# An mLSTM layer that forms the first head's values and gate columns ahead of its first queries, keys and output gates

## The chip, the cores and the metric

The kernel runs on one core of a Trainium2 chip. The metric is the device time of one execution in microseconds (us); where several runs are given, their median. The core has five engines with an instruction stream each: TensorE (PE in the rows, with its weight loads as PEld), VectorE (DVE), ScalarE (ACT), GpSimd (POOL) and SyncE (SP, which issues the transfers). They wait for one another through semaphores.

## The reference

The program is a trunk of four sub-layers on 1024 tokens of 1024 features: latent attention, a gated MLP, an mLSTM mixer ("matrix memory"), and a gated MLP again, each behind an RMS norm that is scaled and shifted by a conditioning vector. The change lies in the mLSTM mixer. Cut to what matters, it computes

```
proj = h @ w_in                       # h: normed input, 1024 x 1024
q, k, v, o, gates = split(proj)       # 4 heads; q, k 128 wide, v 256 wide a head
i_pre, f_pre = gates                  # one input and one forget gate a head and token
b = cumsum(log_sigmoid(f_pre))        # inside chunks
# a chunk after the other, with state C, n and running maximum m:
dmat  = b[t] - b[s] + i[s]            (causal)
m_t   = max(b + m, max(dmat))
s_mat = (q k^T) * exp(dmat - m_t)
num   = exp(b + m - m_t) * (C q) + s_mat v
den   = the same with n in place of C, and the row sums of s_mat
out   = num / max(|den|, exp(-m_t))
C, n, m = the state after the chunk
y = rms_norm(out) * head_norm * sigmoid(o);   result = y @ w_out
```

Values of all tokens are needed before a chunk's products, and the gates of all four heads come out of the same projection (eight columns of it).

## The kernel before, in words

Every matrix product in full precision is three matmuls (helper `mm3`, lines 178 to 180): the high and the low part of one operand with the high part of the other, and the high part with the low. A weight unit is a block of 128 x 1024 numbers: `unit` (lines 161 to 172) has SP load it into `wraw`, ScalarE copy it to its high part `whi` (line 170) and GpSimd subtract to get the low part `wlo` (line 171). The units' buffers rotate.

Tokens stand in two halves of 512. At the end of the MLP before, `norm_next` (lines 1109 to 1114) norms each half into `h[0]` and `h[1]`. For a half, ones are multiplied with the sums of squares `ssq` on TensorE (`st`, line 247), VectorE forms `var` (line 251), GpSimd `rstd` (line 252), TensorE spreads it over rows (`rb`, line 259), and then VectorE and ScalarE write eight blocks of h (lines 273 to 275). These TensorE steps do not stand where the code calls them. `later(n, step, key)` (line 190) puts a step in a queue, and `mm3` counts it down: the step is emitted after n more calls of `mm3`, that is 3n matmuls. `need(key)` (line 193) emits what is left of a key at once. For the second half `st` comes after W0 = 10 calls, and `rb` three calls later. The gate computation of the first head is placed in the same way by GATES: `gates0` (transposes `gg` of the gate columns `gtok`, then the chain of line 1366 to 1382 on ScalarE and VectorE), `gates1` (`gr`, lines 1386 and 1387), `gates2` (`gp`, line 1399), `gates3` (`gcol`, lines 1414 and 1415).

The mixer of head 0 begins with q, k and o of the first half (`in_proj`, 24 matmuls of 512 columns each, named `inp`), then `need(h[1])`, then q, k, o of the second half (72 matmuls), then eight tiles of values with the gates' columns (`vp`, 24 matmuls of 264 columns each, in the pool psA of four PSUM banks). Every `vp` is split into `va` by ScalarE and VectorE (lines 594, 595), and its last eight columns are copied to `gtok` (line 1345). Then come q and k of head 1 (`nxt = qk(1)`), five pieces of which (QK1) are emitted ahead of `need(gcol)`, and the chain over the chunks of head 0: `po` and `pc` with the state `C` (lines 1291 to 1297), with pieces of other projections between (`cover`), and `yT` at the head's end (line 1323).

All instructions of an engine run in one order, which the tile scheduler fixes when the kernel is built: an instruction stands about where it is emitted, and `tc.high_priority()` moves one ahead of other ready work of its engine.

Of the kernel before, what the change touches and what calls it, by code (L numbers as in the profile page):

```python
# [11 lines left out]
F32 = mybir.dt.float32  # L12
# [6 lines left out]
P = 128  # L19
D = 1024  # L20
S = 1024
KT = D // P
HS = 512
# [6 lines left out]
KSCALE = 128 ** -0.5  # L30
# [5 lines left out]
NT = 2  # L36

DVA = 258
QK1 = 5
SCALE_ACT = ((0, 0), (1, 0), (1, 1))  # L40

STEPS = "nspppnspppoooonmooso", "nnsposppooponpmspoopo"
# [1 line left out]
WARM = 14  # L44
W0, WF = 10, 12
SHARE = 7
GATES = (2, 16, 20, 24)
OUTS = 2
MODS = (0,) * 4 + (3,) + (2,) * 11
MODS_OUT = ((0,) * 5 + (1,) * 3, (1,) * 6 + (0,) * 2)  # L50
# [38 lines left out]
U_MQ, U_MK, U_MV, U_MO, U_MG, U_OUT1 = 0, 4, 8, 16, 24, 25  # L89
U_MV0 = (U_MV, U_MV + 1, U_MG)  # L90
# [10 lines left out]
def trunk_kernel(ctx: ExitStack, tc: tile.TileContext, xT, pos, c_d, cols_d, mod_w, win, winT, w0, w1, wf, wd, out):  # L101
    nc = tc.nc
    PSUM = bass.MemoryType.PSUM
    n_names = [0]

    def nm(s):
        n_names[0] += 1
        return f"{s}_{n_names[0]}"

    act, dve, pool, pe = nc.scalar, nc.vector, nc.gpsimd, nc.tensor  # L110
# [6 lines left out]
    def phase(name, **kw):  # L117
        st = ExitStack()
        p = st.enter_context(tc.tile_pool(name=name, bufs=1, reuse_waits="tile", **kw))
        return st, p  # L120
# [11 lines left out]
    def block(i, shape, dt, name):  # L132
        return blk.tile(shape, dt, tag=f"b{i}", name=nm(name))
# [27 lines left out]
    def mm_tile(name):  # L161
        return psA.tile([P, HS], F32, tag="mm", name=nm(name))


    def unit(src, lo_eng=None, w=1024):
        raw = wp.tile([P, 1024], F32, tag="wraw", bufs=wraws, name=nm("wraw"))[:, 0:w]
        nc.sync.dma_start(raw, src)
        hi = wp.tile([P, 1024], F32R, tag="whi", bufs=wbufs, name=nm("whi"))[:, 0:w]
        lo = wp.tile([P, 1024], F32R, tag="wlo", bufs=wbufs, name=nm("wlo"))[:, 0:w]
        act.activation(hi, raw, AF.Copy)  # L170
        (lo_eng or pool).tensor_tensor(lo, raw, hi.bitcast(F32), ALU.subtract)  # L171
        return hi, lo

    def mm3(ps, ls, rs, first, last, more=False):

        lh, ll = ls
        rh, rl = rs
        pe.matmul(ps, lh, rh, start=first, stop=False, skip_group_check=more)  # L178
        pe.matmul(ps[:, 0:rl.shape[-1]], lh, rl, start=False, stop=False, skip_group_check=more)  # L179
        pe.matmul(ps, ll, rh, start=False, stop=last, skip_group_check=more)  # L180
        for e in list(queue):
            e[0] -= 1
            if e[0] == 0:
                queue.remove(e)
                e[1]()
# [4 lines left out]
    def later(n, fn, key):  # L190
        queue.append([n, fn, key])

    def need(key):

        while any(e[2] is key for e in queue):
            e = next(e for e in queue if e[2] is key)
            queue.remove(e)
            e[1]()
# [94 lines left out]
    def halves(h, hf, k):  # L293
        return h[hf][0][:, k, :], h[hf][1][:, k, :]

    def wk(u, k, w=P):
        return u[0][:, k * w:(k + 1) * w], u[1][:, k * w:(k + 1) * w]
# [14 lines left out]
    h = [[block(2 + i, [P, KT, HS], F32R, "h") for i in range(2)], None]  # L312
# [7 lines left out]
    def small(name):  # L320
        return psS.tile([P, HS], F32, tag="sm", bufs=1, name=nm(name))
# [79 lines left out]
    ps = small("warm")  # L401
# [80 lines left out]
    def in_proj(u, hf):  # L482
        ps = mm_tile("inp")
        for k in range(KT):
            mm3(ps, wk(u, k), halves(h, hf, k), k == 0, k == KT - 1)
        return ps
# [105 lines left out]
    def split_ps(hi, lo, ps, scale=None):  # L592
        if scale is None:
            act.activation(hi, ps, AF.Copy)
            dve.tensor_tensor(lo, ps, hi.bitcast(F32), ALU.subtract)
        else:
            act.activation(hi, ps, AF.Copy, scale=scale)
            dve.scalar_tensor_tensor(lo, ps, scale, hi.bitcast(F32), ALU.mult, ALU.subtract)
# [173 lines left out]
    def piece(gen, n=1):  # L772
        for _ in range(n):
            next(gen, None)
# [3 lines left out]
    def proj_next():  # L778
        for r in proj:
            yield  # L780
            if r is not None:
                args.append(r)
                return
# [7 lines left out]
    for n in range(2 * NH):  # L791
        q, kk, qr, kvu, i, hf, head = args.pop(0)
        nxt = proj_next()
# [36 lines left out]
    def open_ffn(i):  # L830
        stX, px = phase("px", side="right")
        load_cols(i, px)
        stP = ExitStack()
        psC = stP.enter_context(tc.tile_pool(name="psC", bufs=1, space=PSUM, reuse_waits="tile"))
        return stX, px, stP, psC
# [254 lines left out]
    stX, px, stP, psC = open_ffn(1)  # L1090
# [34 lines left out]
    h = hs  # L1125
# [5 lines left out]
    def qk_tiles(hd):  # L1131

        if hd == 1:
            return [[ys[hf][:, t, :] for hf in range(2)] for t in (4, 6)]
        return [[pm.tile([P, HS], F32, tag=f"{t}{hf}", name=nm(t)) for hf in range(2)] for t in ("qT", "kT")]

    def qk_evac(ps, t, hf, scale):
        act.activation(t[hf], ps, AF.Copy, scale=scale)


    uqk = [unit(w1[U_MQ]), unit(w1[U_MK]), unit(w1[U_MO])]
    need(h[0])
    pqk = [in_proj(u, 0) for u in uqk]
    need(h[1])
    stP.close()
    stD.close()
    stX.close()

    stM, pm = phase("pm", side="right")
    stQ = ExitStack()  # L1150
    psD = stQ.enter_context(tc.tile_pool(name="psD", bufs=4, space=PSUM, reuse_waits="tile"))
    def og_evac(ps, m, hf):

        o = ys[hf][:, m, :]
        act.activation(o, ps, AF.Tanh, scale=0.5)
        pool.tensor_scalar(o, o, 0.5, 0.5, ALU.mult, ALU.add)

    ys = [block(XB[hf], [P, KT, HS], F32, "y") for hf in range(2)]
    qT, kT = qk_tiles(0)
    evacs = (lambda ps, hf: qk_evac(ps, qT, hf, 1.0), lambda ps, hf: qk_evac(ps, kT, hf, KSCALE),  # L1160
             lambda ps, hf: og_evac(ps, 0, hf))
    for ps, ev in zip(pqk, evacs):
        ev(ps, 0)
    for u, ev in zip(uqk, evacs):
        ev(in_proj(u, 1), 1)

    R = MH * NC

# [16 lines left out]
    def va_tiles():  # L1185

        hi, lo = [pm.tile([P, 8, w], F32R, tag=f"va{w}", name=nm("va")) for w in (DVA, 256)]
        pool.memset(hi[:, :, 256:DVA].bitcast(F32), 1.0)
        return hi, lo
# [44 lines left out]
    def load_rows(hd, hf):  # L1234

        o = (hd * NC + hf * 4) * P
        e, ib = crow[:, hf * HS:(hf + 1) * HS], pm.tile([P, HS], F32, tag="ib", name=nm("ib"))
        for i, t in enumerate((e, ib)):
            nc.sync.dma_start(t, g_d[i][:, o:o + HS].broadcast_to([P, HS]))
        grows.append((e, ib))  # L1240
# [86 lines left out]
    def run(gen):  # L1327
        while True:
            try:
                next(gen)  # L1330
            except StopIteration as e:
                return e.value


    gtok = pm.tile([P, 2 * MH, NC], F32, name="gtok")
    va = va_tiles()
    uv = [unit(w1[i]) for i in U_MV0]
    for t in range(8):
        ps = mm_tile("vp")
        tsl = slice((t % 4) * P, (t % 4 + 1) * P)  # L1340
        for k in range(KT):
            mm3(ps[:, 0:264], (h[t // 4][0][:, k, tsl], h[t // 4][1][:, k, tsl]), wk(uv[k // 3], k % 3, 264),
                k == 0, k == KT - 1)
        split_ps(va[0][:, t, 0:256], va[1][:, t, :], ps[:, 0:256])
        dve.tensor_copy(gtok[:, :, t], ps[:, 256:264])
    g1, g2 = crow[0:R, 0:4 * P], crow[0:R, 4 * P:8 * P]
    gi, gf, gb, gc = [g1[:, i * P:(i + 1) * P] for i in range(4)]
    ga, gu, gw, gl = [g2[:, i * P:(i + 1) * P] for i in range(4)]
# [8 lines left out]
    gcol = pm.tile([P, 4 * R], F32, name="gcol")  # L1357
# [53 lines left out]
    def gates3():  # L1411
# [5 lines left out]
        for hf in range(2):  # L1417
            load_rows(0, hf)

    for n, gate_step in zip(GATES, (gates0, gates1, gates2, gates3)):  # L1420
        later(n, gate_step, gcol)
    nxt = qk(1)
    piece(nxt, QK1)
    need(gcol)

    def gcl(kind, hd, c):
# [4 lines left out]
    for hd in range(MH):  # L1431
        pre, obs = [], []
        if hd == 0:
            steps = prep(hd, qT, kT, pre)
            next(steps)
            piece(nxt)
            run(steps)
            cover = (r for gen in (ogate(hd), nxt) for r in gen)
        else:
            vs = v_proj(hd) if hd > 1 else vs  # L1440
            va = next(vs)
            if hd > 1:
                piece(vs, 2)
            steps = prep(hd, qT, kT, pre)
            next(steps)
            piece(vs)
            run(steps)
            run(vs)
            cover = ogate(hd)
        for _ in chain(hd, pre, va, obs):  # L1450
            piece(cover)
        run(cover)
        if hd == 0:
            vs = v_proj(1)
            piece(vs, 2)
        elif hd < MH - 1:
            nxt = qk(hd + 1)
            piece(nxt, 2)
        finish(hd, obs)
        if hd < MH - 1:  # L1460
            run(nxt)
            qT, kT = qks.pop()
# [4 lines left out]
    stX, px, stP, psC = open_ffn(2)  # L1467
# [124 lines left out]
```

## Time and profile before

| | us |
|---|---|
| median of 3 runs | 2378.07 (2377.34 to 2380.62) |
| profiled execution, device time | 2385.82 |
| span in its profile | 2384.10 |
| TensorE busy in the span | 2276.5 (95%) |
| its idle in head 0's start, 1216.4 to 1336.1: `gr` | 4.0 |
| same stretch, `po` behind `C` | 1.9 and 0.6 |

The profile is one execution, whose time is 7.75 us over the median of the runs; a difference that is worked out from its rows is added to the median. Rows of the trace come in five views. The page gives totals. The waits view gives what an engine waited for: the engine and line that waited, the releaser behind the arrow, the sum, the number and the longest in us. The windows view gives busy time of each engine in a stretch. The timeline has one instruction a row, in brackets the idle time before it on its engine and what ended it. The transfer view lists the issues in a stretch.

### The profile page before, as it was taken

To read this page: it belongs to the slowest core of one execution; us is meant where nothing else is said; L and a number is where in the kernel's file an instruction comes from. 1 tells how busy PE (TensorE), PEld (TensorE's weight loads), DVE (VectorE), ACT (ScalarE), POOL (GpSimd) and SP (SyncE) were. 2 spreads that over 40 slices of the span, in tenths; PEclk is the share of its full clock that TensorE was granted. 3 is DMA by queue.
4 is the path that set the end of the run, shared out by engine and by line. 5 is a ranking of instruction groups with operands and counts; after the bars stand their busy time and mean duration, and the time that the engine had idled before them with its cause. 6 is when DMAs were issued, how large, how long until landed. Compare 5 with 4: busy or idle time off the path is not lost. (4 is left out here: it accounts for less than half of the span.)

```text
span 2384.1 us, 29447 instructions
## 1 busy us (share of the span) xinstructions
PE 2276.5 (95%) x10861; PEld 1897.2 (80%) x10861; DVE 1505.3 (63%) x2171; ACT 997.8 (42%) x1720; POOL 925.0 (39%) x626
## 2 busy tenths in 40 slices
PE   8999999997999999999999999999799999999997
PEld 6778888775788888788888888978578888878787
DVE  7777777589667666667864525366966666642515
ACT  5356556344444444433234324343444444442312
POOL 4221121435333333666532222234433333365644
PEclk8999999998999999999999999999899999999998
DMA  7512334833322222878652111163232222274533
GB/s 283 151 43 68 93 102 152 291 101 100 102 86 80 80 80 72 270 245 276 202 175 76 54 36 54 41 199 120 71 111 84 80 81 83 79 226 125 183 89 115
DMA packets 112896, 295.72 MB, mean 124 GB/s; under 512 B 13104, under 2 KB 16880, under 8 KB 112752
## 3 DMA queue, kind: packets, MB, share of 16 engines
q1 hardware_dynamic: 112752, 293.84, 38.5%
q8 instruction: 86, 1.41, 0.2%
q14 instruction: 58, 0.48, 0.1%
HBM read 246.70 MB, written 44.47 MB: 122 GB/s over the span
## 5 line engine op out<-in xcount | busy, mean ns | idle before, releaser
L171 POOL TENSOR_TENSOR wlo<-wraw,whi 128x1024 fp32r<-128x1024 f32 (+1 forms) x168 | 402.5, 2398 | 472.2 <-ACT whi L170 416.0
L170 ACT ACTIVATE whi<-wraw 128x1024 fp32r<-128x1024 f32 (+1 forms) x171 | 172.6, 1009 | 358.7 <-PE dn L179 159.0
L938 POOL TENSOR_TENSOR wlo<-raw,whi 128x512 fp32r<-128x512 f32 x132 | 195.7, 1487 | 276.7 <-ACT whi L937 267.7
L180 PE MATMUL dn<-u,wlo 128*128 128x512 f32 (+1 forms) x752 | 285.3, 379 | 1.3 <-POOL wlo L171 1.3
L178 PE MATMUL dn<-u,whi 128*128 128x512 f32 (+1 forms) x752 | 285.9, 380 | 0.0
L179 PE MATMUL dn<-u,whi 128*128 128x512 f32 (+1 forms) x752 | 285.4, 380 | 0.0
L178 PE MATMUL pa<-T,whi 128*128 128x512 f32 x528 | 210.7, 399 | 16.6 <-DVE a L1015 15.3
L179 PE MATMUL pa<-T,whi 128*128 128x512 f32 x528 | 210.1, 398 | 0.0
L180 PE MATMUL pa<-T,wlo 128*128 128x512 f32 x528 | 209.6, 398 | 0.0
L938 POOL TENSOR_TENSOR wlo<-wsum,whi 128x512 fp32r<-128x512 f32 x88 | 121.4, 1382 | 222.4 <-ACT whi L937 222.4
L180 PEld LDWEIGHTS dn<-u,wlo 128*128 128x128 f32 x752 | 143.3, 191 | 28.4 <-POOL wlo L171 1.5
L937 ACT ACTIVATE whi<-wsum 128x512 fp32r<-128x512 f32 x176 | 108.3, 627 | 137.3 <-PE pa L179 62.5
L178 PEld LDWEIGHTS dn<-u,whi 128*128 128x128 f32 x752 | 143.5, 191 | 26.7
L179 PEld LDWEIGHTS dn<-u,whi 128*128 128x128 f32 x752 | 143.3, 191 | 26.5
L291 DVE SCALAR_TENSOR_TENSOR x<-dn,modc,x 128x512 f32<-128x512 f32 (+1 forms) x104 | 73.2, 705 | 140.8 <-PE dn L180 140.7
L178 PEld LDWEIGHTS pa<-T,whi 128*128 128x128 f32 x528 | 101.0, 191 | 42.3 <-DVE a L1015 17.8
L240 DVE TENSOR_TENSOR ssq<-ssq,sq 128x512 f32<-128x512 f32 (+1 forms) x74 | 96.3, 1301 | 46.8 <-ACT sq L238 46.4
L179 PEld LDWEIGHTS pa<-T,whi 128*128 128x128 f32 x528 | 101.2, 192 | 22.8 <-POOL T L886 0.4
L180 PEld LDWEIGHTS pa<-T,wlo 128*128 128x128 f32 x528 | 101.1, 191 | 22.4
L977 ACT ACTIVATE ct<-a,cols 128x512 f32<-128x512 f32 x88 | 71.0, 811 | 107.2 <-DVE a L997 63.8
L937 ACT ACTIVATE whi<-raw 128x512 fp32r<-128x512 f32 x132 | 79.6, 621 | 73.0 <-PE pb L179 57.3
L951 DVE TENSOR_TENSOR wsum<-raw 128x512 f32<-128x512 f32 x44 | 49.0, 1113 | 91.9 <-POOL wlo L938 63.6
(349 smaller groups left out, 5933.4 us busy)
## 6 DMA issues: line engine op xcount, KB each, us to landing
raw<-in_wf SPq DMA_DIRECT2D x96, 512.0 KB, 3.8
wraw<-in_w SPq DMA_DIRECT2D x67, 512.0 KB, 3.8
wraw<-in_wd SPq DMA_DIRECT2D x64, 512.0 KB, 3.6
mraw<-in_mod_w SPq DMA_DIRECT2D x56, 512.0 KB, 4.8
ud<-ct SPq DMA_DIRECT2D x88, 256.0 KB, 2.7
ur<-ud SPq DMA_DIRECT2D x88, 256.0 KB, 4.0
wraw<-in_wd SPq DMA_DIRECT2D x40, 384.0 KB, 3.1
pa<-in_mod_w SPq DMA_DIRECT2D x24, 512.0 KB, 3.8
```

The source lines that it names most:

```text
L170: act.activation(hi, raw, AF.Copy)
L171: (lo_eng or pool).tensor_tensor(lo, raw, hi.bitcast(F32), ALU.subtract)
L178: pe.matmul(ps, lh, rh, start=first, stop=False, skip_group_check=more)
L179: pe.matmul(ps[:, 0:rl.shape[-1]], lh, rl, start=False, stop=False, skip_group_check=more)
L180: pe.matmul(ps, ll, rh, start=False, stop=last, skip_group_check=more)
L240: pin(eng.tensor_tensor(self.t, self.t, sq, ALU.add))
L291: dve.scalar_tensor_tensor(x, ps, g, x, ALU.mult, ALU.add)
L937: act.activation(hi, src, AF.Copy)
L938: eng.tensor_tensor(lo, src, hi.bitcast(F32), ALU.subtract)
L951: dve.tensor_tensor(g["s"], g["rg"][:, 0:HS], g["rg"][:, HS:], ALU.add)
L977: act.activation(t, a[:, 2:], AF.Identity, bias=col(f"cb{l}", m), scale=cw(m, 2))
```

## The change

The three units of values and gate columns and the unit of q are loaded first. The four value tiles of the first token half are formed ahead of everything else and stay in the four banks of psA; q of the first half follows, in a bank of the pool psC that the MLP before had. After `need(h[1])` and the evacuation of that q come the four value tiles of the second half, and behind them q of the second half, both halves of k, and both of o. The five pieces of head 1's queries ahead of `need(gcol)` go (QK1), and three pieces stand in the first step of head 0 (`piece(nxt, 3)`) in place of all that is left. GATES counts anew, from the last value tile on, and the gate steps and the copies to `gtok` are emitted under `high_priority`. No product is added or removed.

```diff
-QK1 = 5
-GATES = (2, 16, 20, 24)
+GATES = (4, 22, 27, 31)
-    uqk = [unit(w1[U_MQ]), unit(w1[U_MK]), unit(w1[U_MO])]
+    def v_gates(t):
+        ps = mm_tile("vp")
+        tsl = slice((t % 4) * P, (t % 4 + 1) * P)
+        for k in range(KT):
+            mm3(ps[:, 0:264], (h[t // 4][0][:, k, tsl], h[t // 4][1][:, k, tsl]), wk(uv[k // 3], k % 3, 264),
+                k == 0, k == KT - 1)
+        return ps
+
+    uv = [unit(w1[i]) for i in U_MV0]
+    uq = unit(w1[U_MQ])
     need(h[0])
-    pqk = [in_proj(u, 0) for u in uqk]
+    vps = [v_gates(t) for t in range(4)]
+    ps = psC.tile([P, HS], F32, tag="up", bufs=4, name=nm("inp"))
+    for k in range(KT):
+        mm3(ps, wk(uq, k), halves(h, 0, k), k == 0, k == KT - 1)
     need(h[1])
-    for ps, ev in zip(pqk, evacs):
-        ev(ps, 0)
-    for u, ev in zip(uqk, evacs):
-        ev(in_proj(u, 1), 1)
+    qk_evac(ps, qT, 0, 1.0)
+    stP.close()
     for t in range(8):
-        ps = mm_tile("vp")
...
+        ps = vps[t] if t < 4 else v_gates(t)
         split_ps(va[0][:, t, 0:256], va[1][:, t, :], ps[:, 0:256])
-        dve.tensor_copy(gtok[:, :, t], ps[:, 256:264])
+        with tc.high_priority():
+            dve.tensor_copy(gtok[:, :, t], ps[:, 256:264])
+    def first_of_all(step):
+        with tc.high_priority():
+            step()
+
     for n, gate_step in zip(GATES, (gates0, gates1, gates2, gates3)):
-        later(n, gate_step, gcol)
+        later(n, lambda gate_step=gate_step: first_of_all(gate_step), gcol)
+    qk_evac(in_proj(uq, 1), qT, 1, 1.0)
+    u = unit(w1[U_MK])
+    for hf in range(2):
+        qk_evac(in_proj(u, hf), kT, hf, KSCALE)
+    u = unit(w1[U_MO])
+    for hf in range(2):
+        og_evac(in_proj(u, hf), 0, hf)
     nxt = qk(1)
-    piece(nxt, QK1)
     need(gcol)
-            piece(nxt)
+            piece(nxt, 3)
```

What this moves on the engines, at the three places of which the prediction speaks. A row is line, operation, out<-in (with the buffers' numbers) and shape; one line number of the changed kernel is one less than that of the kernel before, up to the mixer. TensorE at the sums of squares of the second half; h_1550 and h_1551 are the high and low part of the first half, whi and wlo those of a weight unit. Before:

```order
L178 MATMUL inp_1682_10198<-h_1550_9498,whi_1676_10163 128x512
L179 MATMUL inp_1682_10198<-h_1551_9499,whi_1676_10163 128x512
L180 MATMUL inp_1682_10198<-h_1550_9498,wlo_1677_10164 128x512
L247 MATMUL st_1683_10205<-ones_75,ssq_1622_9887 128x1 x4
L178 MATMUL inp_1682_10198<-h_1550_9498,whi_1676_10163 128x512
L179 MATMUL inp_1682_10198<-h_1551_9499,whi_1676_10163 128x512
```

Changed:

```order
L177 MATMUL vp_1685_10204<-whi_1673_10157,h_1550_9498 128x264
L178 MATMUL vp_1685_10204<-wlo_1674_10158,h_1550_9498 128x264
L179 MATMUL vp_1685_10204<-whi_1673_10157,h_1551_9499 128x264
L246 MATMUL st_1686_10211<-ones_75,ssq_1622_9887 128x1 x4
L177 MATMUL vp_1685_10204<-whi_1673_10157,h_1550_9498 128x264
L178 MATMUL vp_1685_10204<-wlo_1674_10158,h_1550_9498 128x264
```

`st` stands behind 30 matmuls of the mixer in both, and `rb` nine matmuls further on; before they have 512 columns, now 264.

VectorE around `var`, the step between `st` and `rstd`; lines 202 and 201 are products for the conditioning of a later layer with rows from memory (`mraw`), lines 207 and 206 add their bias. Before:

```order
L202 SCALAR_TENSOR_TENSOR mraw_1663_10109,modc1_80<-mraw_1663_10109,crow_66 128x1024
L202 SCALAR_TENSOR_TENSOR mraw_1669_10141,modc1_80<-mraw_1669_10141,crow_66 128x1024
L207 SCALAR_TENSOR_TENSOR modc1_80<-modc1_80,cols1_4405 128x8
L251 TENSOR_SCALAR var_1684_10210<-st_1683_10205 128x4
L273 SCALAR_TENSOR_TENSOR nt_1687_10228<-x_1499_9166,modc1_80,rb_1686_10223 128x512
```

Changed:

```order
L201 SCALAR_TENSOR_TENSOR mraw_1663_10109,modc1_80<-mraw_1663_10109,crow_66 128x1024
L201 SCALAR_TENSOR_TENSOR mraw_1669_10141,modc1_80<-mraw_1669_10141,crow_66 128x1024
L250 TENSOR_SCALAR var_1687_10216<-st_1686_10211 128x4
L206 SCALAR_TENSOR_TENSOR modc1_80<-modc1_80,cols1_4405 128x8
L272 SCALAR_TENSOR_TENSOR nt_1690_10234<-x_1499_9166,modc1_80,rb_1689_10229 128x512
```

`var` moves ahead of the bias, and stays behind both products.

TensorE around `gr`, the first step that needs the whole gate chain; the numbers behind `inp` tell tiles apart. Before:

```order
L178 MATMUL inp_1729_10700<-h_1670_10151,whi_1725_10650 128x512
L179 MATMUL inp_1729_10700<-h_1671_10152,whi_1725_10650 128x512
L180 MATMUL inp_1729_10700<-h_1670_10151,wlo_1726_10651 128x512
L1386 MATMUL gr_1730_10725<-ident_70,crow_66 1x32
L1387 MATMUL gr_1730_10725<-ident_70,crow_66 1x32
L178 MATMUL inp_1734_10742<-h_1550_9498,whi_1732_10738 128x512
```

Changed:

```order
L177 MATMUL inp_1718_10556<-h_1550_9498,whi_1716_10552 128x512
L178 MATMUL inp_1718_10556<-h_1551_9499,whi_1716_10552 128x512
L1389 MATMUL gr_1720_10601<-ident_70,crow_66 1x32
L1390 MATMUL gr_1720_10601<-ident_70,crow_66 1x32
L179 MATMUL inp_1718_10556<-h_1550_9498,wlo_1717_10553 128x512
L177 MATMUL inp_1718_10556<-h_1550_9498,whi_1716_10552 128x512
```

Before, two whole projections (48 matmuls of 512 columns) stand between the last value tile and `gr`; now the second half of q (24) and 14 matmuls of the first half of k, 38 in all. The two transposes `gg` stand 6 and 9 matmuls behind the last value tile in both.

## Rows read from the trace of the kernel before

**Rows 1.** The page: span, and busy time of each engine with its share and instructions.
```profile
span 2384.1 us, 29447 instructions
PE 2276.5 (95%) x10861; PEld 1897.2 (80%) x10861; DVE 1505.3 (63%) x2171; ACT 997.8 (42%) x1720; POOL 925.0 (39%) x626
```
**Rows 2.** Waits of TensorE from 1270 to 1340 us: releaser, us in total, times, longest.
```profile
PE gr L1386 <- DVE crow L1382: 4.0, 1, 4.0
PE po L178 <- ACT C L1296: 1.9, 1, 1.9
PE po L179 <- DVE C L1297: 0.6, 1, 0.6
```
**Rows 3.** Windows: us, busy (instructions) of PE, PEld, DVE, ACT, POOL, granted clock, DMA.
```profile
1250.50:1273.70 23.20, 23.20 (x194) 23.20 (x193) 3.53 (x14) 5.79 (x11) 3.41 (x3) 1.00 0.12 39
1273.70:1289.05 15.35, 11.39 (x52) 8.78 (x50) 7.31 (x13) 9.44 (x14) 9.07 (x4) 1.00 0.37 104
1289.50:1293.00 3.50, 3.50 (x10) 2.67 (x10) 0.59 (x6) 0.00 (x0) 0.00 (x0) 0.51 0.40 150
1323.70:1327.10 3.40, 3.40 (x10) 2.66 (x9) 0.59 (x2) 0.61 (x3) 0.00 (x0) 0.50 0.00 0
```
**Rows 4.** Timeline, TensorE and VectorE at the second half's sums of squares.
```profile
1216.40 0.39 PE L178 MATMUL inp<-h,whi 128*128 128x512 f32 x1
1223.23 0.95 PE L247 MATMUL st<-ones,ssq 128*128 128x1 f32 x8
1224.04 0.47 PE L178 MATMUL inp<-h,whi 128*128 128x512 f32 x1
1218.87 1.93 DVE L240 TENSOR_TENSOR ssq<-ssq,sq 128x512 f32<-128x512 f32 x1 [0.76 <-ACT sq L238]
```
**Rows 5.** Timeline, VectorE, GpSimd and TensorE from the last product to the row sums.
```profile
1222.89 1.23 DVE L202 SCALAR_TENSOR_TENSOR mraw<-mraw,crow 128x1024 f32<-128x1024 f32 x1 [0.95 <-DMA mraw<-in_mod_w]
1224.24 0.15 DVE L251 TENSOR_SCALAR var<-st 128x4 f32<-128x4 f32 x1
1224.48 1.01 POOL L252 TENSOR_TENSOR rstd<-var,nhalf 128x4 f32<-128x4 f32 x1 [4.23 <-DVE var L251]
1226.21 0.60 PE L259 MATMUL rb<-ident,rstd 128*128 128x128 f32 x4
```
**Rows 6.** Waits of TensorE from 2240 to 2250 us, at the last norm of the program.
```profile
PE rb L259 <- POOL rstd L252: 2.2, 1, 2.2
```
**Rows 7.** Windows behind that wait, and behind a wait of 4.6 us in the MLP.
```profile
2248.80:2252.20 3.40, 3.35 (x10) 2.87 (x11) 1.66 (x3) 1.06 (x1) 0.15 (x1) 0.51 0.02 5
1720.70:1726.40 5.70, 5.70 (x14) 4.50 (x15) 5.70 (x10) 3.94 (x6) 0.00 (x0) 0.50 0.07 28
```
**Rows 8.** Waits of TensorE from 1700 to 1725 us, the one ahead of that window.
```profile
PE pa L178 <- DVE a L1015: 4.6, 1, 4.6
```
**Rows 9.** Timeline, TensorE, ScalarE, VectorE and GpSimd in the gate chain.
```profile
1273.69 0.39 PE L178 MATMUL inp<-h,whi 128*128 128x512 f32 x1
1281.02 1.06 ACT L170 ACTIVATE whi<-wraw 128x1024 fp32r<-128x1024 f32 x1 [2.42 <-DMA wraw<-in_w]
1285.33 0.28 DVE L1378 TENSOR_TENSOR crow<-crow 32x128 f32<-32x128 f32 x1
1286.16 2.40 DVE L1381 TENSOR_TENSOR crow<-crow 32x128 f32<-32x128 f32 x1
1286.09 2.34 POOL L171 TENSOR_TENSOR wlo<-wraw,whi 128x1024 fp32r<-128x1024 f32 x1 [1.53 <-ACT whi L170]
1289.07 0.18 PE L1386 MATMUL gr<-ident,crow 32*1 32x32 f32 x1 [3.98 <-DVE crow L1382]
```
**Rows 10.** Transfers issued from 1275 to 1282 us, and from 1253 to 1258 us.
```profile
wraw<-in_w SPq DMA_DIRECT2D x2, 512.0 KB, 4.6
...
wraw<-in_w SPq DMA_DIRECT2D x1, 512.0 KB, 3.6
```
**Rows 11.** Timeline, TensorE in the second half of head 1's chain.
```profile
1384.57 0.38 PE L178 MATMUL po<-C,qw 128*128 128x258 f32 x1 [0.89 <-ACT C L1296]
```

More of the change, by code (lines that the diff above doesn't have):

```diff
@@ L1138, in qk_evac @@
         act.activation(t[hf], ps, AF.Copy, scale=scale)
-    uqk = [unit(w1[U_MQ]), unit(w1[U_MK]), unit(w1[U_MO])]
+    def v_gates(t):
[7 more added lines that the diff above has]
+    uq = unit(w1[U_MQ])
     need(h[0])
-    pqk = [in_proj(u, 0) for u in uqk]
+    vps = [v_gates(t) for t in range(4)]
+    ps = psC.tile([P, HS], F32, tag="up", bufs=4, name=nm("inp"))
+    for k in range(KT):
+        mm3(ps, wk(uq, k), halves(h, 0, k), k == 0, k == KT - 1)
     need(h[1])
-    stP.close()
     stD.close()
@@ L1149, in trunk_kernel @@
     stM, pm = phase("pm", side="right")
-    stQ = ExitStack()
-    psD = stQ.enter_context(tc.tile_pool(name="psD", bufs=4, space=PSUM, reuse_waits="tile"))
     def og_evac(ps, m, hf):
@@ L1159, in trunk_kernel @@
     qT, kT = qk_tiles(0)
-    evacs = (lambda ps, hf: qk_evac(ps, qT, hf, 1.0), lambda ps, hf: qk_evac(ps, kT, hf, KSCALE),
-             lambda ps, hf: og_evac(ps, 0, hf))
-    for ps, ev in zip(pqk, evacs):
-        ev(ps, 0)
-    for u, ev in zip(uqk, evacs):
-        ev(in_proj(u, 1), 1)
+    qk_evac(ps, qT, 0, 1.0)
+    stP.close()
+    stQ = ExitStack()
+    psD = stQ.enter_context(tc.tile_pool(name="psD", bufs=4, space=PSUM, reuse_waits="tile"))
     R = MH * NC
@@ L1336, in trunk_kernel @@
     va = va_tiles()
-    uv = [unit(w1[i]) for i in U_MV0]
     for t in range(8):
-        ps = mm_tile("vp")
[L1340 to L1343, printed above, removed]
+        ps = vps[t] if t < 4 else v_gates(t)
         split_ps(va[0][:, t, 0:256], va[1][:, t, :], ps[:, 0:256])
-        dve.tensor_copy(gtok[:, :, t], ps[:, 256:264])
+        with tc.high_priority():
+            dve.tensor_copy(gtok[:, :, t], ps[:, 256:264])
     g1, g2 = crow[0:R, 0:4 * P], crow[0:R, 4 * P:8 * P]
```

## The prediction

> **What bounds the kernel now.** I read the page first: TensorE is busy for 2276.5 of 2384.1 us, and no other engine for more than 63% [rows 1]. The change adds and removes no matmul, so it can only move what TensorE loses: time in which it waits, and time in which it runs at the lower of its two clock levels. The stretch that is rewritten runs from the first matmul of the mixer at 1216.40 [rows 4] to the end of head 0. The second view is therefore TensorE's waits in it. There are two of weight: 4.0 us at `gr`, for the end of the gate chain, and 1.9 us at a `po` that waits for the state C, with 0.6 us more two matmuls later [rows 2]. The third view is the granted clock in windows. Right behind each of the two waits TensorE runs at 0.51 and 0.50 for some 3.5 us, which is 1.2 in place of 2.4 GHz [rows 3]; at half pace 3.4 to 3.5 us do the work of 1.7, so each costs 1.7 us. Of about 10 us lost here, 4.0 + 1.7 stand at `gr` and 1.9 + 0.6 + 1.7 in head 0's chain. Ahead of `gr` TensorE loses nothing: the 23.2 us of value tiles are busy throughout at clock 1.00 [rows 3].
>
> **What the change does, part by part.** The profiled execution is the ledger: 2384.1 us of span, 2385.82 of device time. The runs' median is 2378.07, and I add the sum to that.
>
> First, **`st` comes too early.** 30 matmuls stand ahead of it in both kernels. With 512 columns they took from 1216.40 to 1223.23, 6.83 us, or 0.228 each [rows 4]. With 264 columns a matmul takes 23.20 / 194 = 0.120 [rows 3], so TensorE arrives at 1216.40 + 3.6 = 1220.0. The sums of squares are finished on VectorE at 1218.87 + 1.93 = 1220.8 [rows 4]. TensorE waits 0.8 us where it waited for nothing. VectorE has no other order ahead of that step, so this term is firm to some tenths.
>
> Second, **`rb` comes too early.** The `st` matmuls take 0.8 (1223.23 to 1224.04) [rows 4], nine short matmuls 1.1, so TensorE reaches `rb` at 1222.7. What it needs is `var` on VectorE and `rstd` on GpSimd. `var` stays queued behind the second of two products for the conditioning, which itself waits for its transfer and ends at 1222.89 + 1.23 = 1224.1 [rows 5]. Passing the bias (the order shows it) gains `var` 0.1. `rstd` came 0.24 behind the start of `var` and took 1.01 [rows 5], so it ends near 1225.4, and TensorE waits 2.7 us where before `rb` at 1226.21 waited for nothing. Bounds: had the transfer come at once, 0.95 less [rows 5]; a slower one would add as much. I take 2.7. Behind it the clock should fall: at the program's last norm TensorE waits 2.2 us for the same operand [rows 6] and then runs 3.4 us at 0.51 [rows 7]. That is 1.7 us more. A further wait could follow: the fifth value tile needs a bank of the first four, which VectorE splits only behind its norm of the second half. That norm begins about 1 us sooner than before, and what TensorE loses above it would otherwise have spent waiting there; I cost it at nothing, with 0.6 us as the upper bound.
>
> Third, **`gr`.** From the start of the projection that follows the last value tile to `gr`, the gate chain took 1273.69 to 1289.07, 15.4 us [rows 9]. In that stretch before TensorE had 52 matmuls and 11.4 us of work [rows 3]. Now it has 38 long matmuls and the two `gg`: 38 x 0.228 + 0.4 = 9.1 us. If the chain keeps its length, the wait is 15.4 - 9.1 = 6.3 us. Does it? The copies and steps are under high priority, but on ScalarE and VectorE the chain already ran as soon as its operands were there; what lengthened it were two strangers. ScalarE, in order, waited 2.42 us for a weight transfer ahead of the chain's logarithm [rows 9]; the transfers of that moment needed 4.6 us (median of two), another a little earlier 3.6 [rows 10]. The same pattern (a unit's copy between the chain's two functions) is in the changed program. And VectorE's line 1381 took 2.40 us where a sister operation on the same tile took 0.28, exactly while GpSimd split a unit, 1286.09 to 1288.43 [rows 9]. I let that stand and take 1.0 off for a transfer of common length: chain 14.4, wait 5.3, that is +1.3 over before. Bounds: 6.3 (+2.3) and 15.4 - 2.4 - 2.1 - 9.1 = 1.8 (-2.2).
>
> On the second stranger the Trainium skill has a rule: SBUF — State Buffer, section Who interferes with whom, says that a VectorE operation with two inputs in SBUF contends with a GpSimd operation that reads SBUF, and that who issues first holds the shared ports for a whole instruction while the other blocks. The row agrees: GpSimd started 0.07 us sooner, and 2.40 against 0.28 is its whole length. By that rule the 2.1 us hang on which of two instructions comes first, so with VectorE first the sum below would be lower by 2.1.
>
> Fourth, **the clock behind `gr`.** Behind a wait of 4.0 it was low for 3.5 us [rows 2, 3]; behind one of 4.6 in the MLP [rows 8] for 5.7 [rows 7]. For 5.3 I take the middle, 4.6 us, half of which is 2.3 and 0.6 more than before. Bounds: 0 and 2.85 - 1.7 = 1.15.
>
> Fifth, **head 0's chain.** In the changed order each chunk of head 0 has twelve matmuls of a whole projection as cover, as the later heads have, and head 1's queries and the output gates are spread evenly. Where the later heads stand so, the wait for C in their second half is 0.89 us [rows 11]. I take that: 1.9 becomes 0.9 (-1.0), the 0.6 goes, and with it the low clock, 1.7, in all -3.3. Bounds: 0, if the wait recurs with its clock, since the order of VectorE and GpSimd there is about the same; and -4.2, if all goes.
>
> The other moves cost nothing that I can find: q of the first half lies in a bank that the MLP has left, and the units' loads keep their rotation, with 264-column tiles taking three units where long ones take one for half the time.
>
> **Sum:** 0.8 + 2.7 + 1.7 + 1.3 + 0.6 - 3.3 = +3.8 us, 2378.07 + 3.8 = 2381.9.
>
> **The rivals.**
>
> *Slower: the gate chain keeps its 15.4 us.* The chain is bound by table loads, a transfer and one collision, none of which the change takes out, and TensorE has 2.3 us less to do beside it than before (9.1 for 11.4). Then `gr` waits 6.3, the clock behind it is low for 5.7 us, and the sum is 0.8 + 2.7 + 1.7 + 2.3 + 1.15 - 3.3 = +5.4: 2383.4. If head 0's wait recurs too, it is +8.7: 2386.8. It decides from a wait at `gr` of about 6 us. For it speaks that every step of the chain is the same, against it that two of them were lengthened by chance.
>
> *The same, a little better: both strangers stay away.* Chain 10.9, wait 1.8 at `gr`, and no low clock behind it: 0.8 + 2.7 + 1.7 - 2.2 - 1.7 - 3.3 = -2.0: 2376.1. With the collision alone gone, +1.7: 2379.8 (that is the case in which VectorE issues first). Against the full case speaks that transfers and splits run in the same rhythm as before.
>
> *Faster.* As the last, and the product's transfer ahead of `var` comes 0.95 sooner, so that `rb` waits 1.75 and no low clock follows: -2.0 - 0.95 - 1.7 = -4.65, 2373.4, and a few tenths more where all of head 0's wait goes. Against it: the shortest wait of this stretch with a low clock behind it, 1.9 us [rows 2, 3], is hardly longer.
>
> *The change doesn't do what it says:* were `st` and `rb` moved back behind long matmuls by the scheduler, the first terms (5.2) would go, and the sum be -1.4. The order shows them behind short ones, so I give it nothing.
>
> **How the numbers follow.** A measurement of this kernel can tell about 0.2%, 4.8 us, from no change: 2373.3 to 2382.8 counts as the same. The forecast has 0.50; its own spread (some tenths at `st`, 0.95 at `rb`, 1 at `gr`) puts 0.07 of that over the line. The slower rival has 0.30, the better one 0.14, the faster one 0.06. So faster 0.06, same 0.43 + 0.14 = 0.57, slower 0.37. The range reaches from 2374, just above the faster rival, to 2387, the upper end of the slower one.
>
> **What would show it.** In the profile of the changed kernel TensorE should wait some 0.8 us at `st` near 1220 and 2.7 at `rb` until about 1225.5, with a granted clock near 0.5 behind; 5.3 at `gr` (4 to 6.3) near 1265, with low clock behind; and in head 0 a `po` waiting 0.9 with clock 1.00 after it. The first `yT`, behind all of this, should come 3 to 4 us later than before. I am wrong if `rb` doesn't wait (then `var` is not held by the product), if `gr` waits under 3 us (then the strangers made the chain), or if head 0 keeps a wait of 1.9 (then the cover was not what it lacked).

## The result

The changed kernel takes 2385.01 us (median of 12 runs, 2379.57 to 2388.36), the kernel before 2377.72 in the same series: a ratio of 1.0026 with a 95% interval of 1.0014 to 1.0038, or 6.2 us slower (3.3 to 9.0). The forecast was 3.8 us slower, 2381.9, with a range up to 2387. Two later series of the same kernel gave 1.0016 (1.0006 to 1.0026) and 1.0018 (1.0006 to 1.0030), 3.8 and 4.3 us. The three intervals overlap from 3.3 to 6.2 us. That the kernel is slower is clear of the noise; whether by more than the 0.2% (4.8 us) at which the prediction drew its line is left open.

The profiled execution has a span of 2384.2 us against 2384.1 before [rows 1]. These two don't show the difference, because parts of the program that the change doesn't touch vary by more. The mixer's first matmul came at 1216.40 before and at 1217.57 after; in the other traces of these kernels it came at 1211.65 (before), 1218.70 and 1208.47 (changed). So I compare the stretch that is rewritten, from that matmul to the first `yT`. It took 1336.14 - 1216.40 = 119.7 us in the first trace of before and 118.3 in a second; in three of the changed kernel it took 121.7, 121.5 and 123.4. The means are 119.0 and 122.2, 3.2 us more. That lies inside the intervals of the two later series and just under the lower edge of the first.

TensorE's waits in the stretch after the change (engine and line, releaser, us in total, times, longest); [rows 2] has those of before:

```profile
PE gr L1389 <- DVE crow L1385: 4.4, 1, 4.4
PE st L246 <- DVE ssq L239: 2.0, 1, 2.0
PE rb L258 <- POOL rstd L251: 1.2, 1, 1.2
PE po L177 <- ACT C L1303: 0.8, 1, 0.8
```

The two waits at `st` and `rb` are new, `gr` still waits, and of the waits in head 0's chain one short one is left. The windows of this kernel show the clock behind them (us, busy time of PE, PEld, DVE, ACT, POOL with instructions, granted clock, DMA share, GB/s):

```profile
1217.57:1339.29 121.72, 113.15 (x640) 98.21 (x639) 56.64 (x133) 48.73 (x98) 32.70 (x24) 0.96 0.23 72
1226.60:1230.00 3.40, 3.20 (x15) 3.21 (x16) 1.85 (x3) 1.27 (x2) 0.28 (x2) 0.50 0.00 0
1266.40:1270.90 4.50, 4.50 (x13) 3.09 (x14) 1.53 (x10) 1.08 (x4) 0.00 (x0) 0.50 0.28 107
1319.60:1323.00 3.40, 3.31 (x16) 2.75 (x17) 1.79 (x3) 2.45 (x6) 2.41 (x1) 1.00 0.34 136
```

Behind `rb` and behind `gr` TensorE ran at the lower level, 1.2 GHz, for 3.2 us from `rb`'s start and 4.6 us from `gr`'s (the windows shown lie inside these times); behind the remaining `po` it ran at 2.4. [rows 3] has the two windows of before, behind `gr` and behind `po`.

Waits and low clock account for the whole stretch. Take from it TensorE's waits of over 0.2 us and half of the time that it then ran at the lower level: in each of the twelve traces of this document 109.2 to 109.9 us are left, for stretches from 111.4 to 123.4. In the first two traces that is 119.7 - 6.7 - 3.4 = 109.6 before and 121.7 - 8.5 - 3.9 = 109.3 after.

The waits at the start, and what released them, on the timeline of the changed kernel:

```profile
1219.25 1.06 ACT L169 ACTIVATE whi<-wraw 128x1024 fp32r<-128x1024 f32 x1 [3.48 <-DMA wraw<-in_w]
1220.21 0.61 ACT L237 ACTIVATE sq<-x 128x512 f32<-128x512 f32 x1
1220.38 2.36 POOL L170 TENSOR_TENSOR wlo<-wraw,whi 128x1024 fp32r<-128x1024 f32 x1 [3.48 <-ACT whi L169]
1220.86 2.43 DVE L239 TENSOR_TENSOR ssq<-ssq,sq 128x512 f32<-128x512 f32 x1 [1.60 <-ACT sq L237]
1223.35 1.05 PE L246 MATMUL st<-ones,ssq 128*128 128x1 f32 x8 [2.00 <-DVE ssq L239]
1225.50 0.15 DVE L250 TENSOR_SCALAR var<-st 128x4 f32<-128x4 f32 x1
1226.80 1.11 PE L258 MATMUL rb<-ident,rstd 128*128 128x128 f32 x4 [1.20 <-POOL rstd L251]
```

ScalarE had the last square of the norm behind the copy of a weight unit, and that copy waited 3.48 us for its transfer. The last sum on VectorE then took 2.43 us beside GpSimd's split of that unit. The same sum without a split beside it took 0.69, here at an earlier norm:

```profile
434.89 0.69 DVE L239 TENSOR_TENSOR ssq<-ssq,sq 128x512 f32<-128x512 f32 x1 [0.28 <-ACT sq L237]
```

So the sums ended late, `st` waited longer than forecast and `rb` less. The second of the products ahead of `var`, by contrast, had its transfer at once. In the second and third trace of the same kernel the waits are 0.5 and 2.3, and 0.4 and 2.3; the sum took 1.7 and 1.6 there, again beside a split. At 0.69 it would have ended before TensorE came to `st` in both, and 0.2 us after in the first (an estimate from these durations; no run took the split away here).

### The profile page after: what moved, and what is told of

It is laid out like the page before. It is cut to its first block, busy times and chain, and to the rows that moved or that the text cites. A ratio compares the mean times of both kernels' runs of the same rounds, so it can differ in the third digit from the quotient of the medians.

```text
span 2384.2 us, 29448 instructions
## 1 busy us (share of the span) xinstructions
PE 2273.7 (95%) x10861; PEld 1894.6 (79%) x10861; DVE 1511.7 (63%) x2171; ACT 997.4 (42%) x1720; POOL 926.4 (39%) x626
## 5 line engine op out<-in xcount | busy, mean ns | idle before, releaser
L177 PE MATMUL pa<-T,whi 128*128 128x512 f32 x528 | 210.6, 399 | 16.3 <-DVE a L1014 15.1
L937 POOL TENSOR_TENSOR wlo<-wsum,whi 128x512 fp32r<-128x512 f32 x88 | 121.5, 1383 | 220.9 <-ACT whi L936 216.9
```

Of the source, the lines that this page charges most:

```text
L937: eng.tensor_tensor(lo, src, hi.bitcast(F32), ALU.subtract)
```

## The experiments

All runs are held against the kernel before, in its runs of the same series; the stretch is the one above.

**The changed kernel again, twice.** No edit.

> The changed kernel once more, for its time and a second trace. Its first trace puts only +2.0 us into the stretch from the mixer's first matmul to the first yT (121.7 us against 119.7 before), while its runs are 6 us slower. Theory A (the loss sits in this stretch, and the first trace was a good one for it): the second trace shows the stretch at 123 us or more, through a longer gr wait or a longer low clock. Theory B (the stretch costs 2 us, and the rest of the 6 is scatter of the runs): the stretch is again within 1 us of 121.7, and the new ratio to before lies nearer 1.001 than 1.0026.

> The changed kernel a third time, on the chip of best2. Its stretch is 121.7 and 121.5 us against 119.7 and 118.3 of the kernel before: 1.8 to 3.4 us; its runs were 6.2 and 3.8 us slower. If the stretch is all that differs, the ratio here lies between 1.0004 and 1.0018 as well as in the interval of the second series, and best2 is 7 to 9 us faster than it; if the changed kernel loses further time elsewhere, the ratio is 1.0025 or more again, and its trace shows more time than before's 226 to 227.5 between the first and the last yT, or ahead of the mixer.

The first gave 2381.47 us, ratio 1.0016 (1.0006 to 1.0026), and a stretch of 121.5 us; the second 2382.77, 1.0018 (1.0006 to 1.0030), and 123.4. Theory B held for the first repetition's stretch. The second's is what Theory A described, longer through the wait at `gr`, at a ratio on the upper edge of what was expected (1.0018). So both occur, and the second shows what differs from one execution to the next. Its waits:

```profile
PE gr L1389 <- DVE crow L1385: 5.8, 1, 5.8
PE rb L258 <- POOL rstd L251: 2.3, 1, 2.3
PE po L177 <- ACT C L1303: 0.8, 1, 0.8
PE st L246 <- DVE ssq L239: 0.4, 1, 0.4
```

and ScalarE in its gate chain, where the copy of a weight unit stands between the two table loads:

```profile
1247.37 1.28 ACT L1371 ACT_TABLE_LOAD   x1
1251.10 1.06 ACT L169 ACTIVATE whi<-wraw 128x1024 fp32r<-128x1024 f32 x1 [2.13 <-DMA wraw<-in_w]
1252.17 1.28 ACT L1373 ACT_TABLE_LOAD   x1
```

The transfer that ScalarE waited for came 2.13 us late here and 0.68 in the first trace, and the wait at `gr` is 5.8 for 4.4. Its trace has 226.2 us from the first `yT` to the first one of the last head (before: 227.5 and 226.4), and its mixer begins earlier than in either trace of before, so nothing points to a loss outside the stretch.

**The kernel before again.** No edit.

> The kernel before once more, for a second trace. The changed kernel's two traces give 121.7 and 121.5 us for the stretch from the mixer's first matmul to the first yT, and the one of before 119.7. If the stretch is reproducible, it lies between 119.2 and 120.2 here, and the difference of the runs over about 2 us is scatter outside the stretch; if the first trace of before was a slow one for it (its weight transfer ahead of the gate chain was late, 2.42 us of wait), it is 117.5 to 118.5, and the loss in the stretch is 3 to 4 us, as the runs say.

2378.04 us in one run, and a stretch of 118.3. Its waits were the same as before to 0.1 us (`gr` 4.0, `po` 1.9, 0.5 and 0.3), and the same transfer was late (2.44 us). What differs is the clock behind the `po`, which stayed high:

```profile
1317.40:1321.00 3.60, 3.52 (x17) 2.89 (x18) 1.33 (x3) 1.27 (x4) 0.00 (x0) 1.00 0.12 49
```

The 1.4 us between the two stretches are the low clock of the first, 3.4 us at 0.50 [rows 3]. A wait of 1.9 us is followed by the lower level in one execution and not in another.

**`st` and `rb` later.**

```diff
-W0, WF = 10, 12
+W0, WF = 18, 12
-                 W0 if hf else None)
+                 W0 if hf else None, 5 if hf else AFTER_RSTD)
```

(the second number is handed on to `rstd_later` as its `turn`)

> The changed kernel with only st and rb of the second half moved back, behind 54 and 69 value matmuls in place of 30 and 39, so that both operands are there when TensorE arrives. Theory 1 (the waits at st and rb, 3.2 us, and the low clock behind, 1.6, are a real loss): they vanish and the time falls by 4 to 5 us against the changed kernel. Theory 2 (they only move: the norm of the second half starts no earlier, and the fifth value tile needs a bank that is split behind that norm): st and rb wait for nothing, but TensorE waits 4 to 5 us at the fifth value tile near 1237 to 1241, low clock follows there, and the time stays within 1.5 us of the changed kernel.

2383.07 us, ratio 1.0021 (1.0004 to 1.0037), and 1.6 us over the changed kernel in the same series; stretch 121.9. Theory 2: no wait at `st` or `rb`, and in their place one of 4.0 at the fifth value tile.

```profile
PE gr L1389 <- DVE crow L1385: 4.4, 1, 4.4
PE vp L177 <- ACT va L593: 4.0, 1, 4.0
PE po L177 <- ACT C L1303: 0.9, 1, 0.9
```

Then it ran at 0.52 from 1237.00 to 1240.50. The loss at the mixer's start is therefore not one of where `st` and `rb` stand. TensorE has about as much work on the first half as before (96 short and 24 long matmuls for 72 long ones), but what comes next needs a bank that is split only behind the norm.

**And another bank for the fifth tile.** On top of the last edit:

```diff
-    stP.close()
-    stQ = ExitStack()
-    psD = stQ.enter_context(tc.tile_pool(name="psD", bufs=4, space=PSUM, reuse_waits="tile"))
+    vps.append(v_gates(4, psC.tile([P, HS], F32, tag="up", bufs=4, name=nm("vp"))))
...
-        ps = vps[t] if t < 4 else v_gates(t)
+        ps = vps[t] if t < 5 else v_gates(t)
```

(`v_gates` takes the bank as its second argument; psC is closed and psD opened behind the split of the fifth tile)

> As late_st (st and rb behind 54 and 69 short matmuls, where they wait for nothing), and the fifth value tile goes to a bank of psC that is free, in place of a bank of the first four tiles. In late_st the wait of 3.2 us at st and rb came back as one of 4.0 us at that tile, released by a split behind the norm of the second half. Theory 1 (the bank is what holds it): the 4.0 us go to under 1, and the stretch from the mixer's first matmul to the first yT falls from 121.7 to 117 or 118 us. Theory 2 (the norm itself is the limit: it ends about 22 us behind the mixer's start, and TensorE has only 17 us of work on the first half): the fifth tile waits 1 to 2 us for blocks of h, the sixth tile again for a bank, and the stretch falls by no more than 2 us.

2380.42 us, ratio 1.0004 (0.9990 to 1.0019); stretch 121.4. Neither theory: the wait at the value tiles fell to 0.7 us, as theory 1 had it, and the stretch hardly fell. The view of waits, and the windows of the gate chain and behind `gr`:

```profile
PE gr L1392 <- DVE crow L1388: 5.8, 1, 5.8
PE po L177 <- ACT C L1301: 0.9, 1, 0.9
PE vp L177 <- DVE gtok L1347: 0.7, 1, 0.7
```

```profile
1249.12:1264.17 15.05, 9.26 (x43) 6.93 (x41) 7.17 (x13) 8.84 (x13) 9.04 (x4) 0.97 0.38 115
1264.20:1273.50 9.30, 9.30 (x24) 6.01 (x25) 2.70 (x15) 1.74 (x6) 0.00 (x0) 0.50 0.38 110
```

In this execution the transfer in the gate chain was late (ScalarE waited 2.08 us), the chain took 15.05 us, `gr` waited 5.8, and the clock stayed low for 9.4 us behind it, where it had done so for 4.6. That is 1.4 us of wait and 2.4 of clock given back in this one trace. The runs, which don't hang on one transfer, are better than the changed kernel's by 1.2 to 2.2 parts in a thousand, but the intervals overlap, so a gain from the bank alone is not shown by the time.

**Gate steps without priority.**

```diff
     def first_of_all(step):
-        with tc.high_priority():
-            step()
+        step()
```

> The changed kernel with the four gate steps emitted without priority, so that they stand where GATES says: gr behind 93 matmuls of 512 columns in place of 38. Theory 1 (gr is early, not the gate chain late): its wait of 4.4 us and the low clock behind it (2.3 us) vanish, head 0's chain still finds its operands in time, and the time falls by 5 to 7 us against the changed kernel, to about the kernel before or a little under. Theory 2 (the chain's end is needed at the same time anyway, by the score products and the rows read back from memory): the gr wait goes, but a wait of 3 to 6 us appears at the first po or st of head 0, and the time stays within 2 us.

2376.64 us, ratio 0.9994 (0.9981 to 1.0007), and 4.8 us under the changed kernel in the same series; stretch 117.3. `gr` now stands behind 66 matmuls, not the 93 of the expectation, which counted the projections wrongly; the reading is not touched by it. Theory 1, with one part given back:

```profile
PE po L177 <- ACT C L1303: 2.5, 2, 1.6
PE rb L258 <- POOL rstd L251: 2.4, 1, 2.4
PE gr L1389 <- DVE crow L1385: 0.9, 1, 0.9
PE st L246 <- DVE ssq L239: 0.4, 1, 0.4
```

The wait at `gr` fell from 4.4 to 0.9 and the clock behind it was 1.00; a wait of 1.6 at head 0's second chunk is new. 3.5 + 2.3 - 1.6 = 4.2 us, and the stretch is 4.4 shorter than the mean of the first two traces (121.6).

**Both.** The last two edits together.

> bank together with no_prio (gate steps without priority, gr behind 66 matmuls of 512 columns). no_prio alone has a stretch of 117.3 us, with 2.8 us of waits at st and rb and 1.6 of low clock left in it. If bank's gain adds to it, the stretch is about 113.5 us, and the time 5 to 7 us under the kernel before; if the norm is the limit, 115.5 to 117, and the time within 2 us of no_prio.

2375.73 us, ratio 0.9990 (0.9979 to 1.0002); stretch 114.0, with the clock at its upper level throughout. The gains add up in the stretch. The runs show 2.4 us under the kernel before, short of the 5 to 7 expected.

**Both, and the gate steps a little sooner.** GATES = (2, 20, 24, 28) on top.

> best with GATES (2, 20, 24, 28) in place of (4, 22, 27, 31): the gate chain starts six matmuls sooner, and gr stands behind 60 matmuls in place of 66. best has a stretch of 114.0 us, with waits of 0.7 at a value tile, 1.0 at gr, 1.7 and 0.8 at po, and no low clock. If the gate chain's end sets the first po, its wait of 1.7 goes down and the stretch ends at 112.5 to 113.5; if VectorE's queue of weights and score products ahead of the state sets it, the stretch stays at 114 and only gr's wait changes, within 0 to 1.5 us. Against the kernel before (118.3 and 119.7) the runs should be 4 to 6 us faster; best's were 2.4, with an interval from 5 faster to 0.5 slower.

2372.03 us, ratio 0.9971 (0.9956 to 0.9986): 6.9 us faster than the kernel before and some 11 faster than the changed one in the same series, for which 7 to 9 were expected. The stretch, 111.4, is even under what was expected: the first `po` waits for nothing, and neither does `gr`.

```profile
PE po L177 <- ACT C L1301: 0.9, 1, 0.9
PE vp L177 <- DVE gtok L1347: 0.7, 1, 0.7
```

```profile
1209.98:1321.36 111.38, 109.68 (x640) 95.62 (x639) 56.29 (x133) 48.69 (x98) 32.76 (x24) 1.00 0.24 78
```

Against the 121.7 of the first trace after, with 113.15 busy at a mean clock of 0.96, this has the same 640 matmuls in 109.68 us. In this trace the transfer in the gate chain was only 0.75 us late; had it been 2.1, as in the third trace of the changed kernel, `gr` would have waited about 1 us (an estimate: a chain of 15.1 us there, 14.1 here).

**The kernel before with later gate steps.** GATES = (2, 21, 25, 29) in place of (2, 16, 20, 24).

> The kernel before with GATES (2, 21, 25, 29) in place of (2, 16, 20, 24): gr stands behind 60 long matmuls in place of 48. By the row of before (chain 15.4 us, wait 4.0) the wait at gr falls to about 1.2 us and no low clock follows: 2.8 + 1.7 = 4.5 us faster than before, if gcol is not needed sooner. Rival: the first score products and the rows read back are then late, and give back all of it; then a wait of 2 to 4 us appears at the first po of head 0.

2374.45 us, ratio 0.9988 (0.9976 to 1.0000): 2.9 us faster, where 4.5 were forecast; stretch 115.1, which is 3.2 and 4.6 under the two traces of before. No wait at `gr` and no low clock there. Not all is gain: `po` waits 1.2 for the score product (0.3 before), and the wait for C is still there, with low clock behind it:

```profile
PE po L178 <- ACT C L1296: 2.1, 1, 2.1
PE po L178 <- ACT pT L1228: 1.2, 1, 1.2
```

```profile
1315.70:1319.10 3.40, 3.33 (x10) 2.89 (x11) 0.93 (x3) 1.29 (x4) 0.00 (x0) 0.50 0.07 28
```

The gate chain was shorter than forecast as well. The transfer between its table loads was 0.90 us late in place of 2.42, and ScalarE made the next unit's copy behind the chain. Then GpSimd's split was not beside line 1381, and VectorE's operation took what its sisters take ([rows 9] has 2.40 us for it):

```profile
1282.51 0.28 DVE L1381 TENSOR_TENSOR crow<-crow 32x128 f32<-32x128 f32 x1
1283.97 2.38 POOL L171 TENSOR_TENSOR wlo<-wraw,whi 128x1024 fp32r<-128x1024 f32 x1 [3.07 <-ACT whi L170]
```

**Less cover in head 0.** piece(nxt, 6) in place of 3 in the changed kernel.

> The changed kernel with piece(nxt, 6) in place of 3: three pieces of 12 matmuls less are left to lie between the chunks of head 0, so that the last chunks have the head's next value tiles there as in the kernel before. Theory 1 (the gain in head 0's chain, 3.6 us, comes from more cover): the waits of before at po return, 0.5 to 1.9 us each with a low clock, and the stretch grows from 121.7 to 123 us or more. Theory 2 (it comes from VectorE having no score work queued in the state's way at the middle of the head): the wait of 0.85 us stays, no low clock follows, and the stretch grows by 0.6 us at most, the wait at the last chunk.

2385.95 us in one run; stretch 122.8. By the waits it is theory 2: the one of 0.84 us stays, one of 0.55 at the last chunk comes back (as in before), and the clock behind both is 1.00. The stretch is 1.2 over the mean of the changed kernel's first two traces and lies between the two expectations; the 0.6 us beyond 0.55 are within what traces of one kernel differ by (121.5 to 123.4). So fewer pieces cost the half microsecond of the last chunk, and don't bring back the 1.9. The run can't say more on cover, though: TensorE's order has the same twelve matmuls of a projection ahead of the `po` that waits in all three kernels, before, changed and this one. Only ahead of the last chunk does their cover differ.

## Why the prediction was right or wrong

The sum forecast +3.8; the stretch shows +3.2 between the means of its traces, and the runs 3.8 to 6.2. Term by term, between the mean of two traces before and of three after (us):

| term | forecast | measured |
|---|---|---|
| waits at `st` and `rb` | +3.5 | +2.9 |
| low clock behind them | +1.7 | +2.0 |
| wait at `gr` | +1.3 | +0.9 |
| low clock behind it | +0.6 | +0.6 |
| head 0's chain with its clock | -3.3 | -2.8 |
| rest of the stretch | 0 | -0.4 |

No term is off by more than 0.7 us, and the errors partly cancel.

*The waits at `st` and `rb`*, 0.8 + 2.7 = 3.5. Measured 3.2, 2.7 and 2.6. The sum was near, its division not always: in the first trace `st` waited 2.0 and `rb` 1.2. The term at `st` was called firm because VectorE has no other order there. ScalarE, one step ahead of it, was left out, and so was GpSimd: the row that gave the end of the sums, 1.93 us at 1218.87 [rows 4], is itself three times the 0.69 of a sum with no split beside it. The low clock behind, forecast 1.7, cost 3.2 / 2 = 1.6 in the first trace and 5.3 / 2 = 2.6 in the third, where it lasted 5.3 us from `rb`'s start:

```profile
1217.20:1222.40 5.20, 5.20 (x24) 5.20 (x25) 3.92 (x6) 1.79 (x3) 0.01 (x1) 0.50 0.00 0
```

*What these waits are.* Here the reasoning was incomplete. The prediction charged them to the place of `st` and `rb`, and the last rival said that behind longer work the 5.2 us would go. With `st` and `rb` moved back they came back as 4.0 at the fifth value tile with its low clock. I had seen that wait (for a bank split behind the norm) but costed it only as an addition of up to 0.6; that the two exclude each other, and that without the first the second takes its place in full, I had not worked out.

*`gr`*, +1.3 by a chain of 14.4 and a wait of 5.3. The first trace has a chain of 13.67 (1252.67 to 1266.34) and a wait of 4.4, the third 5.8: the two ends of one transfer that is late or not, and the forecast between them. TensorE's work beside it, forecast 9.1, was 9.2:

```profile
1252.67:1266.34 13.67, 9.22 (x43) 6.93 (x42) 7.20 (x13) 8.86 (x13) 9.07 (x4) 0.92 0.43 121
```

The collision on VectorE recurred in all traces of the changed kernel, one operation earlier in the chain than before (line 1381 here is line 1378 there):

```profile
1262.53 2.34 POOL L170 TENSOR_TENSOR wlo<-wraw,whi 128x1024 fp32r<-128x1024 f32 x1 [0.66 <-ACT whi L169]
1262.65 2.36 DVE L1381 TENSOR_TENSOR crow<-crow 32x128 f32<-32x128 f32 x1
```

With the copy behind the chain (the run with later gate steps in the kernel before) it was gone. So the rule of the Trainium skill that the prediction drew on (SBUF — State Buffer, section Who interferes with whom) agrees in both directions: 2.36 and 2.40 beside a split, 0.28 without.

*The clock behind `gr`*, forecast 2.3, cost 4.6 / 2 = 2.3 in the first trace, 2.5 and 2.1 in the others. Right; but 3.4 us of low clock behind a wait of 4.4 in one kernel (late_st) and 9.4 behind one of 5.8 in another (bank) show how far this term reaches.

*Head 0's chain*, -3.3. The 1.9 became 0.8, with high clock, and the 0.6 went. The size was right against the first trace of before, and about 1.7 too large against its second, in which the low clock didn't follow the wait. The cause was wrong for the larger part. I gave more cover as the reason, and it holds for the 0.6 at the last chunk, which came back with fewer pieces. Ahead of the `po` that waited 1.9 there were twelve matmuls of cover before the change too. What differs there is when C comes: from the fourth chunk's first state product (`pc`) to that `po` it took 9.3 us before and 8.3 after, with 7.4 us of work for TensorE between them in both. In before VectorE had four score operations of 1.25 us in all from 1312.13 on, and ScalarE an exponential, where the changed kernel had none; that is read off the timelines, and no run undid this alone.

What is left of the wait, and the 0.9 of the later heads [rows 11] that the term was taken from, I hadn't asked about. In both kernels VectorE comes to C late because a GpSimd split began 0.06 us ahead of one of its operations (in the changed kernel the third of four scalings `ob`, at 1315.60). First the kernel before, then the changed one, and last the same four operations in the changed kernel with no split beside them:

```profile
1317.19 2.40 POOL L171 TENSOR_TENSOR wlo<-wraw,whi 128x1024 fp32r<-128x1024 f32 x1
1317.25 2.36 DVE L1313 TENSOR_TENSOR s<-s,r 128x4 f32<-128x4 f32 x1 [1.13 <-POOL s L1312]
1319.65 1.46 DVE L1315 TENSOR_SCALAR ob<-ob,s 128x256 f32<-128x256 f32 x4
```

```profile
1314.87 0.16 DVE L1320 TENSOR_TENSOR s<-s,r 128x4 f32<-128x4 f32 x1 [1.13 <-POOL s L1319]
1315.07 3.65 DVE L1322 TENSOR_SCALAR ob<-ob,s 128x256 f32<-128x256 f32 x4
1315.54 2.40 POOL L170 TENSOR_TENSOR wlo<-wraw,whi 128x1024 fp32r<-128x1024 f32 x1 [0.70 <-ACT whi L169]
1331.25 1.14 DVE L1322 TENSOR_SCALAR ob<-ob,s 128x256 f32<-128x256 f32 x4
```

That is 2.5 us in either kernel, more than the wait of 1.9 or of 0.9, and it is so in all twelve traces. The prediction saw this collision in the gate chain alone; the traces have it ahead of `st`, `gr` and this `po`. That the waits at `st` and `po` would go without it is an estimate from these durations; no run moved the split there.

*The rivals.* The slower rival, in which the chain keeps its length, is what one of the three executions did: 5.8 at `gr` is near the 6.3 it gave. It had 0.30, and with the forecast's upper edge 0.37 for slower; given a result on both sides of that line, the split between same and slower was about as uncertain as the prediction had it. The range held the time.

*What wasn't forecast at all* is that the change is a step towards a faster kernel. The prediction priced the gate steps' new place as it stood. No term of it asked what the same order would give with `gr` behind more work: two small edits (where the gate steps stand, a fifth bank with `st` and `rb` later) turn +3.2 us in the stretch into -7.6. Part of that needs no change at all: the kernel before with later gate steps has -3.9, and by the runs the two faster kernels (0.9971 for the last combination, 0.9988 for this one, in different series) are not clearly apart.

## What to carry to other kernels

When a wait is priced by the place of the instruction that waits, look for what is needed next from the same producer: moving the instruction may only move the wait, and the two must not be added. A step that ends a long chain on other engines belongs behind as much of TensorE's work as the chain takes at its longest, late transfers included; giving it priority pulls it to the front of work that would have covered it. When an operation in a chain takes much longer than its sisters, look for what another engine did at that moment, and then look for the same pair elsewhere; here it stood in three places and was priced in one. Waits of some 2 us can cost nearly as much again in clock (1.7 us) or nothing, so two kernels should be compared by the stretch in several traces, not by one span.

## What the runs showed of the hardware

Whether the clock falls behind a wait of about 1.9 us differs between executions of one kernel (0.50 for 3.4 us, and 1.00). In the stretch of the twelve traces, waits of 1.6 and 1.7 (gate steps without priority, alone and with the bank) were followed by 1.00. One of 2.1 (the kernel before with later gate steps), four of 2.3 to 2.5 at `rb`, and those of 4.0 to 5.8 were followed by the lower level. So was one of 1.2, in the changed kernel's first trace, where one of 2.0 had ended some 2 us before it. How long the clock stays low varies as well: 3.4 to 5.0 us behind waits of 4.4, and 4.3 and 9.4 behind two of 5.8.

A VectorE operation of 0.28 us on 32 x 128 numbers takes 2.4 when a GpSimd split of 128 x 1024 that began before it runs beside it. This happened in eleven of the twelve gate chains. The sums of squares ahead of `st` took 1.6 to 2.5 us for 0.69 in the same way in all twelve traces, and in the kernel before a product of 128 x 4 numbers 2.36 for 0.16.
